# A decoder layer on one core: the activated MLP columns transposed by a trip through HBM and by VectorE in 32x32 blocks, and six pairs fewer by seven products

## The chip, the cores and the metric

One core of a Trainium2 chip runs the whole layer in one launch. The metric is the device time in microseconds of one execution; lower is better. The time before is the median of three runs.

## What is computed

A decoder layer over 256 tokens of width 2048, all in float32: two attention groups of eight heads each, an output projection with a residual, and an MLP. The change lies in the MLP alone:

```
h = _rmsnorm(x, norm_mlp_pre[layer])
u = jnp.square(jax.nn.relu(h @ w_up[layer]))
x = x + _rmsnorm(u @ w_down[layer], norm_mlp_post[layer])
```

Here h is 256x2048, `w_up` 2048x8192, u 256x8192 and `w_down` 8192x2048.

## The kernel before

**Exact products by three passes.** Each float32 operand is split into a part `hi` (float32r) and a rest `lo`. A product is three matmuls, hi*hi, hi*lo and lo*hi (`three`), each of 128 stationary columns and 512 moving ones. For each weight tile of 128x1024, ACT writes `hi` and DVE writes `lo` (`split`, and `split_gain` where the weights also take the RMSNorm gain).

**Up.** `w_up` is done in eight rounds j of 1024 columns (`for j in range(FF // CW)`). A round has four accumulators in PSUM, one for each of two token blocks b and two column halves n, and 16 steps over k, the blocks of 128 rows. A plain step ("k") is 4 products, 12 matmuls. Two neighbouring k steps can instead be a pair "by seven" ("w"): a Strassen-Winograd scheme with 7 products where the plain pair has 8. For that DVE forms sums of the weight blocks (`seven`: three additions of 128x1024 or 128x512), four pieces are split, and sums of the left operand are kept in `st` (`left_sums`). The extra products gather in four further banks m, and `close` and four additions bring them back into the accumulators at the round's end. `UP_STEPS` says which steps of a round go by seven, `UP_PAIRS` where the pair's weights are loaded to (`ab` and `ab2` through POOL's DMA queue, or two `raw` buffers through SP's).

**Evacuation of a round.** The down product needs u with its columns on the partitions. `up_evac` does this for each of the four accumulators: ACT writes `r` = Relu of the accumulator times the row scale, TensorE transposes `r` in four blocks of 128x128 into the accumulator's own bank (tile `rt`), and ACT squares that into `uT[j]` (a tile of 128x1024: 4 column blocks by 256 tokens). The banks then serve as m in the next round. For the column blocks in `AWAY`, `lo_away` also sends -hi to HBM by ACT's queue and adds u to it there by POOL's queue; the sum is the `lo` part, fetched again in down.

**Down.** `w_down` is done in two chunks of 1024 output columns, each over 64 k blocks, with the pairs of `DOWN_SEVEN` by seven; pairs in both lists (`SHARED`) form their left sums in the first chunk, keep them in HBM (`keep_s`) and fetch them in the second (`down_back`).

**Order.** The order on each engine and queue is the order of the calls; there is no scheduler. `Flow` keeps a clock that advances by TensorE's work as it is issued. A chain is a generator; `yield d` continues it d us of that clock later, so the delays (`D_UP`, `UP_STEP` and so on) place instructions in the queues of ACT, DVE, SP and POOL; the engines themselves wait for data by semaphores. `Weights.emit` issues loads and splits six tiles ahead of their use (`W_AHEAD`), with five `raw` buffers and eight pairs of hi and lo. Raw weight loads are on SP's queue:

```
raw = self.pool.tile([P, CW], F32, tag="raw", bufs=RAW_BUFS, name=name)
self.nc.sync.dma_start(out=out, in_=src)
```

Of the kernel before, what the change touches and what calls it, by code (L numbers as in the profile page):

```python
# [18 lines left out]
F32 = mybir.dt.float32  # L19
# [7 lines left out]
P = 128  # L27
D = 2048
# [61 lines left out]
D_X0, D_X, D_SS, D_TAB = 8.0, 3.0, 3.0, (14.0, 20.0)  # L90
D_NORM, D_HT, D_SECOND = 4.5, 1.5, 4.0

D_UP, UP_STEP = 1.8, 2.2


SUMS_AHEAD = 2


UP_PAIRS = [()] + [("ab", "ab2", "ab", "ab2")] * 5 + [("ab2", "ab", "raw", "ab"), ("ab", "raw", "raw")]


def up_steps(first, *groups):
# [4 lines left out]


THREE = up_steps(range(6, 11), (11, 12), (13,), (14, 15))
FOUR = up_steps(range(8, 12), (12,), (13,), (14,), (15,))  # L110
UP_STEPS = [up_steps(range(16)), THREE] + [FOUR] * 5 + [THREE]

ST = 13 * 256
N_SEVEN = [sum(w == "w" for w, _ in steps) for steps in UP_STEPS]


DOWN_SEVEN = ((5, 7, 9, 11, 13, 15, 19, 21, 23, 25, 27, 29), range(3, 28, 2))
AWAY = range(4, 14)
LATE = 10
SHARED = [k for k in DOWN_SEVEN[0] if k in DOWN_SEVEN[1]]  # L120
# [145 lines left out]
def layer(nc, tc, io):  # L266
# [13 lines left out]
    def bank(i, name):  # L280
        return ps.tile([P, 512], F32, tag=f"bank{i}", bufs=1, name=name)
# [650 lines left out]

    uT, ukeep = {}, {}

    def up_evac(j, b, i, acc, order):

        yield UP_STEP * order
        r = late["up"].tile([P, 512], F32, tag="r", bufs=2, name=f"r{j}_{b}")
        nc.scalar.activation(r, acc, AF.Relu, scale=rstd2[b])
        yield D_UP if j > 1 else 2 * D_UP  # L940
        t = bank(i, f"rt{j}_{b}")
        for k in range(4):
            transpose(t[:, k * P:(k + 1) * P], r[:, k * P:(k + 1) * P])
        if j not in uT:
            if j in (0, 1, 10, 11, 12, 13):
                t2 = late["u01" if j < 2 else "ab2" if j < 12 else "ab"][:, j % 2 * CW:(j % 2 + 1) * CW]
            else:
                tag = {"tag": "T", "bufs": 2} if j > 13 else {"tag": f"uT{j}", "bufs": 1}
                t2 = late["up"].tile([P, CW], F32, name=f"uT{j}", **tag)
            uT[j] = t2.rearrange("p (k s) -> p k s", k=4)  # L950
        nc.scalar.activation(uT[j][:, :, b * P:(b + 1) * P], t.rearrange("p (k s) -> p k s", k=4), AF.Square)
        if b and j in AWAY:
            flow.start(lo_away(j), 2.0 + 4.0 * (j % 2))

    def lo_away(g):

        ukeep[g] = dram.tile([P, CW], F32, name=f"ukeep{g}")
        u = uT[g].rearrange("p k s -> p (k s)")
        for h in range(2):
            c = slice(h * 512, (h + 1) * 512)  # L960
            t = late["up"].tile([P, 512], F32, tag="r", bufs=2, name=f"neg{g}_{h}")
            nc.scalar.activation(t.bitcast(F32R), u[:, c], AF.Copy, scale=-1.0)
            yield 1.0
            nc.scalar.dma_start(out=ukeep[g][:, c], in_=t)
            yield 7.0
        if g < LATE:
            yield 34.0
        else:
            while not dpl:
                yield 2.0  # L970
            yield 4.0 + 5.0 * (g % 2) + 20.0 * ((g - LATE) // 2)
        for h in range(2):
            c = slice(h * 512, (h + 1) * 512)
            nc.gpsimd.dma_start(out=ukeep[g][:, c], in_=u[:, c], accum_op=OP.add)
            yield 2.0 if g < LATE else 10.0

    def split_u(c, g):
        if (c, g) == (0, 0):
            uh, ul = [wp.tile([P, CW], F32R, tag=w, bufs=W_BUFS, name=f"u{w}0").rearrange("p (k s) -> p k s", k=4)
                      for w in ("hi", "lo")]  # L980
        else:
            uh = dpl["dp"].tile([P, 4, S], F32R, tag="uhi", bufs=2, name=f"uhi{c}_{g}")
            ul = u_lo.pop((c, g), None) or lo_tile(c, g)
        u, h, l = [x.rearrange("p k s -> p (k s)") for x in (uT[g], uh, ul)]
        if c and g or g in AWAY:
            nc.scalar.activation(h, u, AF.Copy)
            if not c:
                load_lo(c, g, ul)
        else:
            split(h, l, u)  # L990
        return uh, ul
# [99 lines left out]
    for j in range(FF // CW):  # L1091
        at = {bn: 4 * (j % 2) + i for i, bn in enumerate(PARTS)}
        if j == 0:
            accs = {bn: acc_bank(f"acc_u0_{bn[0]}{bn[1]}") for bn in at}
            at = {bn: (turn[0] - 3 + i) % 4 for i, bn in enumerate(at)}
        else:
            accs = {bn: bank(i, f"acc_u{j}_{bn[0]}{bn[1]}") for bn, i in at.items()}
        steps = wide_u[j]
        order = in_order(len(steps), (APART[1], 0)) if j == 0 else [(t, b) for t, (w, _, _) in enumerate(steps)
                                                                    for b in range(NB if w == "k" else 1)]  # L1100
        for t, b in order:
            what, k, tiles = steps[t]
            if (j, t, b) == (0, 8, 0):
                flow.finish(*res)
                late["po"].release()
                mix.release()
                late["up"] = pool("up", "right")
                late["st"] = late["up"].tile([P, ST], F32R, tag="st", bufs=1, name="st")
                for n in ("ab", "ab2", "c", "u01"):
                    late[n] = late["up"].tile([P, 2 * CW], F32, name=n)  # L1110
                flow.start(all_sums())
            if (j, t, b) == (FF // CW - 1, 4, 0):
                weights.limit -= 1
                u_next = split_u(0, 0)
            if (j, what, k, b) == (1, "k", 8, 0):
                fourth = flow.start(left_sums(3), 20.0)
            if j == 2 and t == 0:
                flow.finish(fourth)
            if j == 1 and what == "w":
                flow.until(lambda: len(sums) > k)  # L1120
            if what == "k":
                w = weights.get(tiles[0])
                h_done(k, b)
                for n in range(2):
                    c = slice(n * 512, (n + 1) * 512)
                    three(accs[b, n], [tok(hT[x], k, b) for x in range(2)], [w[x][:, 0, c] for x in range(2)], t == 0, t == len(steps) - 1)
                    if j == 0 and t == len(steps) - 1:
                        evac.append(flow.start(up_evac(n, b, at[b, n], accs[b, n], 2 * b + n - 0.25 * (2 * b + n))))
                    flow.pump()
                if b == NB - 1:  # L1130
                    weights.free(tiles[0])
                continue

            first, last = k == 0, k == N_SEVEN[j] - 1
            if first:
                weights.ahead = W_AHEAD
                flow.finish(*evac[-4:])
                m = {n: bank(i, f"m{n}_{j}") for n, i in zip((1, 6, 7, 5), free)}
            blocks = [[tok(hT[x], 2 * k + kk, bb) for x in range(2)] for kk, bb in ((0, 0), (1, 0), (1, 1))]
            if last:  # L1140
                weights.ahead -= 1
            seven_products(tiles, (blocks, sums[k]), accs, m, first, last, last and N_SEVEN[j] > 3)
            if last:
                more = close(closing(), m)
        free = [at[bn] for bn in PARTS]
        if j:

            for bn in PARTS:
                nc.vector.tensor_tensor(out=accs[bn], in0=accs[bn], in1=more[bn], op=OP.add)
            for o, (b, n) in enumerate(PARTS):  # L1150
                evac.append(flow.start(up_evac(2 * j + n, b, at[b, n], accs[b, n], o + 0.6)))
    weights.ahead = W_AHEAD
    u_last = evac[-4:]
    up = late["up"]
# [86 lines left out]
    for c in range(2):  # L1241
# [5 lines left out]
        for t, (what, k, tiles) in enumerate(wide_d[c]):  # L1247
# [31 lines left out]
            if (c, what, k) == (0, "k", 3):  # L1279
                weights.limit += 1  # L1280
            if (c, what, k) == (0, "k", 36):
                g_half = [late["up"].tile([P, 512], F32, tag="r", bufs=2, name=f"g_half{n}") for n in range(2)]
                for n in range(2):
                    load_gain(n, g_half[n])
            if (c, what, k) == (1, "k", 40):
# [39 lines left out]
def arrays_of(inputs):  # L1325

    a = {n: np.ascontiguousarray(inputs[n][0]) for n in ("x", "w_in", "w_uq", "w_ukv", "w_out", "w_up", "w_down")}
    a["xt"] = np.ascontiguousarray(np.concatenate([a["x"], inputs["norm_attn_pre"]]).T)
    a["pos"] = np.ascontiguousarray(inputs["positions"].reshape(NB, P).T)
    a["gains"] = np.ascontiguousarray(np.concatenate(  # L1330
        [inputs[n].reshape(-1, P) for n in ("q_latent_norm", "kv_latent_norm", "norm_mlp_pre")]).T)
    for n in ("norm_attn_post", "norm_mlp_post"):
        a[n] = np.ascontiguousarray(inputs[n])
    a["consts"] = shape_constants()
    return a
# [20 lines left out]
```

## Time and profile before

| | |
|---|---|
| median of three runs | 1046.23 us (1046.1 to 1047.08) |
| the profiled execution | 1045.28 us, of which the span is 1043.5 |
| granted TensorE clock | 0.998 |
| busy: PE, DVE, ACT, POOL | 99%, 81%, 62%, 8% of the span |
| the up rounds | from 368 to 702 us of the span |
| the down chunks | from 702 us on |
| transposes of `r` on PE (`rt`) | 128, between 403.0 and 714.2 us |

The profile is one execution seen by the hardware profiler. PE is TensorE's matmuls, PEld its weight loads, DVE VectorE, ACT ScalarE, POOL GpSimd, SP the engine that issues most of the DMAs. The lines by slices show the busy share of 40 equal parts of the span in tenths. L298 is the matmul helper, L302 the transpose helper, L308 and L309 the two instructions of a split, L312 and L313 those of a split with gain.

### The profile page before, as it was taken

How to read it: one execution, taken by the hardware profiler on the slowest of the kernel's cores; microseconds unless marked ns; L12 is line 12 of the kernel's file. 1: busy time of each engine (PE TensorE's matmuls, PEld its weight loads, DVE VectorE, ACT ScalarE, POOL GpSimd, SP SyncE). 2: the span in 40 equal slices, each digit the busy share in tenths (PEclk: the TensorE clock that was granted, in tenths of full speed). 3: DMA queues.
4: the chain of work that ended last, by engine and by line, in shares of the span. 5: the costliest groups of instructions: out<-in, count | busy, mean ns of one | idle time of the engine just before them, and what ended most of it. 6: DMA issues, size and time to landing. Idle time of an engine off the chain costs nothing.

```text
span 1043.5 us, 13429 instructions
## 1 busy us (share of the span) xinstructions
PE 1033.2 (99%) x4825; PEld 859.5 (82%) x4825; DVE 843.1 (81%) x1132; ACT 641.9 (62%) x876; POOL 79.8 (8%) x121
## 2 busy tenths in 40 slices
PE   9999999999999999999999999999999999999996
PEld 6888889888888888888888888888888888888885
DVE  6676536567547669999999999898998999898795
ACT  6584436565445566665866767666675765766561
POOL 0000000000000000000011101001101001111100
PEclk9999999999999999999999999999999999999999
DMA  9975447454447295646769668489979868888962
GB/s 308 362 233 150 139 131 241 145 162 151 151 148 239 99 350 184 225 150 205 228 213 316 174 245 247 147 289 324 348 255 357 288 226 329 294 313 318 364 223 81
DMA packets 86787, 244.02 MB, mean 234 GB/s; under 512 B 7616, under 2 KB 12224, under 8 KB 86336
## 3 DMA queue, kind: packets, MB, share of 16 engines
q1 hardware_dynamic: 62560, 164.13, 46.0%
q0 software_dynamic: 20848, 73.41, 22.1%
q10 hardware_dynamic: 3312, 5.62, 1.5%
q8 instruction: 38, 0.62, 0.2%
q14 instruction: 29, 0.24, 0.1%
HBM read 220.06 MB, written 23.07 MB: 233 GB/s over the span
## 4 chain that ended last, share of the span: by engine, by line
PE 96%; DVE 1%; issue 1%; DMA 0%; ACT 0%; SPq 0%; POOL 0%; DVEq 0%; POOLq 0%; ACTq 0%
PE y L298 24%; PE acc_u L298 24%; PE acc_o L298 8%; PE m L298 7%; PE md L298 7%; PE acc_v L298 4%; PE acc_qk L298 4%; PE acc_ckv L298 2%; PE acc_ukv L298 2%; PE acc_q L298 2%; PE acc_cq L298 2%; PE acc_k L298 2%; PE acc_uq L298 2%; PE rt L302 1%; PE sc_b L298 1%
## 5 line engine op out<-in xcount | busy, mean ns | idle before, releaser
L309 DVE TENSOR_TENSOR lo<-raw,hi 128x1024 fp32r<-128x1024 f32 (+3 forms) x205 | 231.2, 1148 | 79.3 <-ACT hi L308 78.5
L308 ACT ACTIVATE hi<-raw 128x1024 fp32r<-128x1024 f32 (+3 forms) x205 | 201.5, 996 | 70.7 <-DMA raw<-in_w_in 16.5
L298 PE MATMUL acc_u<-hi,hT_hi 128*128 128x512 f32 x356 | 141.6, 398 | 0.0
L298 PE MATMUL acc_u<-hi,hT_lo 128*128 128x512 f32 x356 | 139.1, 391 | 0.4 <-DVE hT_lo L309 0.4
L298 PE MATMUL acc_u<-lo,hT_hi 128*128 128x512 f32 x356 | 138.8, 390 | 0.0
L298 PE MATMUL y<-hi,uhi 128*128 128x512 f32 x346 | 135.0, 390 | 0.0
L298 PE MATMUL y<-hi,ulo 128*128 128x512 f32 x346 | 134.7, 389 | 0.0
L298 PE MATMUL y<-lo,uhi 128*128 128x512 f32 x346 | 134.6, 389 | 0.0
L313 DVE SCALAR_TENSOR_TENSOR lo<-raw,gcol,hi 128x1024 fp32r<-128x1024 f32 x74 | 92.4, 1279 | 9.6 <-ACT hi L312 9.5
L312 ACT ACTIVATE hi<-raw,gcol 128x1024 fp32r<-128x1024 f32 x74 | 83.0, 1146 | 26.2 <-DMA raw<-in_w_up 13.1
L298 PEld LDWEIGHTS acc_u<-hi,hT_lo 128*128 128x128 f32 x356 | 66.8, 188 | 14.9 <-DVE hT_lo L309 0.9
L298 PEld LDWEIGHTS acc_u<-lo,hT_hi 128*128 128x128 f32 x356 | 67.0, 188 | 12.9
L298 PEld LDWEIGHTS acc_u<-hi,hT_hi 128*128 128x128 f32 x356 | 66.9, 188 | 12.8
L298 PEld LDWEIGHTS y<-hi,uhi 128*128 128x128 f32 x346 | 65.0, 188 | 13.4
L298 PEld LDWEIGHTS y<-hi,ulo 128*128 128x128 f32 x346 | 65.0, 188 | 13.4
L298 PEld LDWEIGHTS y<-lo,uhi 128*128 128x128 f32 x346 | 65.0, 188 | 13.4
L308 ACT ACTIVATE hi<-u 128x1024 fp32r<-128x1024 f32 (+1 forms) x38 | 37.6, 991 | 46.1 <-DVE u L368 30.5
L309 DVE TENSOR_TENSOR lo<-st_down,hi 128x1024 fp32r<-128x1024 f32 x50 | 59.9, 1220 | 1.1 <-ACT hi L308 1.1
L308 ACT ACTIVATE hi<-st_down 128x1024 fp32r<-128x1024 f32 x50 | 52.0, 1049 | 5.8 <-PE y L298 4.1
L298 PE MATMUL md<-hi,s 128*128 128x512 f32 x150 | 54.3, 389 | 0.0
L298 PE MATMUL acc_o<-hi,mixT_hi 128*128 128x512 f32 x128 | 51.8, 405 | 0.0
L298 PE MATMUL acc_o<-hi,mixT_lo 128*128 128x512 f32 x128 | 50.2, 392 | 0.0
(332 smaller groups left out, 2167.7 us busy)
## 6 DMA issues: line engine op xcount, KB each, us to landing
raw<-in_w_down SPq DMA_DIRECT2D x78, 512.0 KB, 6.5
raw<-in_w_up SPq DMA_DIRECT2D x76, 512.0 KB, 5.3
raw<-in_w_in SPq DMA_DIRECT2D x55, 512.0 KB, 4.8
ab<-in_w_up POOLq DMA_DIRECT2D x22, 1024.0 KB, 5.9
raw<-in_w_out SPq DMA_DIRECT2D x32, 512.0 KB, 4.2
ab_down<-in_w_down POOLq DMA_DIRECT2D x13, 1024.0 KB, 9.2
ulo<-ukeep POOLq DMA_DIRECT2D x25, 512.0 KB, 6.0
c<-in_w_down POOLq DMA_DIRECT2D x6, 1024.0 KB, 10.8
```

Source lines behind the costliest of these rows:

```text
L298: nc.tensor.matmul(out, a, b, start=start, stop=stop)
L302: nc.tensor.transpose(out, a, ident)
L308: nc.scalar.activation(hi, src, AF.Copy)
L309: nc.vector.tensor_tensor(out=lo, in0=src, in1=hi.bitcast(F32), op=OP.subtract)
L312: nc.scalar.activation(hi, src, AF.Copy, scale=g)
L313: nc.vector.scalar_tensor_tensor(out=lo, in0=src, scalar=g, in1=hi.bitcast(F32), op0=OP.mult, op1=OP.subtract)
```

## The change

- `up_evac` no longer transposes. After Relu, ACT squares `r` in place in SBUF and writes it to a tile in HBM (`rkeep`, 128 tokens x 512 columns, 256 KB) by its own queue. It then starts `turn_u`.
- `turn_u`, 9 us of the flow's clock later (11 for the last of a round's four), reads that tile back by four DMAs on SP's queue. Each fills 32 partitions: the tokens of a block of 32 go on the partitions and the runs of 128 columns stay whole (512 bytes), so that 32x32 blocks stand where a transpose of each block alone gives the transposed tile. 7 us later VectorE does one transpose of 128x512 in 32x32 blocks into `uT[j]`.
- Each group of 128 columns of u then stands on the partitions in another order, so the rows of `w_down` are permuted likewise on the host.
- Every up round from the second on has three pairs by seven (before: 3, 4, 4, 4, 4, 4, 3), and the first down chunk loses the pair 5. The fourth pair's left sums are no longer made. The space they had is the third buffer of tag `r`, which now holds `r`, the read-back tile `x` and the negated copies of `lo_away` in turn.
- The delays in `lo_away` become shorter (7 to 4 twice, 34 to 26), as it starts later.
- `split_u` waits, in the order of issue, until a tile's transposes have been issued.

```
-D_UP, UP_STEP = 1.8, 2.2
+UP_STEP = 2.4
+D_BACK, D_TURN, D_LO, D_ADD = 9.0, 7.0, 4.0, 26.0
...
-UP_PAIRS = [()] + [("ab", "ab2", "ab", "ab2")] * 5 + [("ab2", "ab", "raw", "ab"), ("ab", "raw", "raw")]
+UP_PAIRS = [(), *[("ab", "ab2", "ab"), ("ab2", "ab", "ab2")] * 2, ("ab", "ab2", "ab"), ("ab2", "ab", "raw"),
+            ("ab", "raw", "raw")]
...
 THREE = up_steps(range(6, 11), (11, 12), (13,), (14, 15))
-FOUR = up_steps(range(8, 12), (12,), (13,), (14,), (15,))
-UP_STEPS = [up_steps(range(16)), THREE] + [FOUR] * 5 + [THREE]
-
-ST = 13 * 256
+UP_STEPS = [up_steps(range(16))] + [THREE] * 7
+
+ST = 10 * 256
...
-DOWN_SEVEN = ((5, 7, 9, 11, 13, 15, 19, 21, 23, 25, 27, 29), range(3, 28, 2))
+DOWN_SEVEN = ((7, 9, 11, 13, 15, 19, 21, 23, 25, 27, 29), range(3, 28, 2))
...
-    def up_evac(j, b, i, acc, order):
+    def up_evac(j, b, acc, order):
 
         yield UP_STEP * order
-        r = late["up"].tile([P, 512], F32, tag="r", bufs=2, name=f"r{j}_{b}")
+        r = late["up"].tile([P, 512], F32, tag="r", bufs=3, name=f"r{j}_{b}")
         nc.scalar.activation(r, acc, AF.Relu, scale=rstd2[b])
-        yield D_UP if j > 1 else 2 * D_UP
-        t = bank(i, f"rt{j}_{b}")
-        for k in range(4):
-            transpose(t[:, k * P:(k + 1) * P], r[:, k * P:(k + 1) * P])
+        nc.scalar.activation(r, r, AF.Square)
+        keep = dram.tile([P, 512], F32, name=f"rkeep{j}_{b}")
+        nc.scalar.dma_start(out=keep, in_=r)
+        flow.start(turn_u(j, b, keep), D_BACK + 2.0 * (b and j % 2))
+
+    turned = set()
+
+    def turn_u(j, b, keep):
+
+        x = late["up"].tile([P, 512], F32, tag="r", bufs=3, name=f"x{j}_{b}")
+        back = keep.rearrange("(q t) (a c) -> a t q c", q=4, a=4)
+        for a in range(4):
+            nc.sync.dma_start(out=x[32 * a:32 * a + 32].rearrange("t (q c) -> t q c", q=4), in_=back[a])
+        yield D_TURN
...
-        nc.scalar.activation(uT[j][:, :, b * P:(b + 1) * P], t.rearrange("p (k s) -> p k s", k=4), AF.Square)
-        if b and j in AWAY:
-            flow.start(lo_away(j), 2.0 + 4.0 * (j % 2))
+        nc.vector.transpose(uT[j][:, :, b * P:(b + 1) * P].rearrange("p k (q t) -> p k q t", q=4),
+                            x.rearrange("p (q k c) -> p k q c", q=4, k=4))
+        if b:
+            turned.add(j)
+            if j in AWAY:
+                flow.start(lo_away(j), 1.0)
...
-            yield 7.0
+            yield D_LO
         if g < LATE:
-            yield 34.0
+            yield D_ADD
...
     def split_u(c, g):
+        flow.until(lambda: g in turned)
...
-            if (j, what, k, b) == (1, "k", 8, 0):
-                fourth = flow.start(left_sums(3), 20.0)
-            if j == 2 and t == 0:
-                flow.finish(fourth)
...
+    a["w_down"] = np.ascontiguousarray(
+        a["w_down"].reshape(FF // 512, 4, 4, 32, D).transpose(0, 2, 1, 3, 4).reshape(FF, D))
```

More of the change, by code (lines that the diff above doesn't have):

```diff
@@ L960, in lo_away @@
             c = slice(h * 512, (h + 1) * 512)
-            t = late["up"].tile([P, 512], F32, tag="r", bufs=2, name=f"neg{g}_{h}")
+            t = late["up"].tile([P, 512], F32, tag="r", bufs=3, name=f"neg{g}_{h}")
             nc.scalar.activation(t.bitcast(F32R), u[:, c], AF.Copy, scale=-1.0)
@@ L1127, in layer @@
                     if j == 0 and t == len(steps) - 1:
-                        evac.append(flow.start(up_evac(n, b, at[b, n], accs[b, n], 2 * b + n - 0.25 * (2 * b + n))))
+                        evac.append(flow.start(up_evac(n, b, accs[b, n], 0.75 * (2 * b + n))))
                     flow.pump()
@@ L1150, in layer @@
             for o, (b, n) in enumerate(PARTS):
-                evac.append(flow.start(up_evac(2 * j + n, b, at[b, n], accs[b, n], o + 0.6)))
+                evac.append(flow.start(up_evac(2 * j + n, b, accs[b, n], o + 0.6)))
     weights.ahead = W_AHEAD
@@ L1281, in layer @@
             if (c, what, k) == (0, "k", 36):
-                g_half = [late["up"].tile([P, 512], F32, tag="r", bufs=2, name=f"g_half{n}") for n in range(2)]
+                g_half = [late["up"].tile([P, 512], F32, tag="r", bufs=3, name=f"g_half{n}") for n in range(2)]
                 for n in range(2):
```

## The prediction

> **What bounds the kernel now.** I read the page first, then TensorE's waits, then the chain in order of time, and last the stage around the change, round by round.
>
> ```profile
> span 1043.5 us, 13429 instructions
> PE 1033.2 (99%) x4825; PEld 859.5 (82%) x4825; DVE 843.1 (81%) x1132; ACT 641.9 (62%) x876; POOL 79.8 (8%) x121
> PE   9999999999999999999999999999999999999996
> DVE  6676536567547669999999999898998999898795
> DMA  9975447454447295646769668489979868888962
> ```
>
> The share for DVE, 81%, is a mean over two halves. In the attention half it is idle for a third or more of the time; in the MLP half, where the change lies, it shows nines. PE shows nines everywhere but at the very end. So I ask what PE waited for:
>
> ```profile
> PE warm L523 <- DVE zero L520: 1.2, 1, 1.2
> PE acc_u L298 <- DVE hT_lo L309: 0.4, 1, 0.4
> PE qrt L302 <- DVE qT L774: 0.2, 1, 0.2
> ```
>
> That is the whole list: 1.8 us, none of it inside the up rounds or the down chunks. There the time is what PE issues; an instruction taken off PE shortens the run by its own time, until another engine cannot follow.
>
> The chain gives the price of a matmul and the length of a round:
>
> ```profile
> 525.19 9.52 PE acc_u L298 x42
> 568.07 9.52 PE acc_u L298 x42
> 610.93 9.52 PE acc_u L298 x42
> 653.79 9.52 PE acc_u L298 x42
> 859.10 27.20 PE y L298 x120
> ```
>
> 27.20/120 = 0.2267 us for a matmul of 512 columns. The run of 42 stands at the same place of each round, so a round of four products-by-seven lasts 42.86 us. It has 16 x 12 - 4 x 3 = 180 matmuls, 40.80 us. The other 2.06 us are its 16 transposes, in four groups, and what they disturb. The same chain inside a round shows two groups themselves:
>
> ```profile
> 577.60 0.44 PE rt L302 x4
> 580.12 0.59 PE rt L302 x4
> ```
>
> **The change part by part.**
>
> *128 transposes leave PE* (32 groups of four). By the shorter group, 32 x 0.44 = 14.1 us; by what a round lasts beyond its matmuls, 8 x 2.06 = 16.5 us, which also holds the slightly slower matmuls between the groups. I take 16.5, since the round is measured whole, and keep 14.1.
>
> *Six pairs return from seven products to eight.* The rounds of before have 0, 3, 4, 4, 4, 4, 4, 3 such pairs, those of after 0 and seven times 3: five fewer. Down's first chunk loses pair 5. Each gives back one product of three passes: 6 x 3 x 0.2267 = +4.1 us.
>
> *The evacuation on ACT.* Before, Relu and a Square out of PSUM; now Relu, a Square in SBUF and a DMA issue.
>
> ```profile
> L939 ACT ACTIVATE r<-acc_u,rstd_pre 128x512 f32<-128x512 f32 x4 | 2.6, 688 | 3.4 <-DVE acc_u L1149 3.4
> L962 ACT ACTIVATE neg<-uT 128x512 fp32r<-128x512 f32 x4 | 2.5, 623 | 1.4 <-DMA ukeep<-neg 1.4
> L951 ACT ACTIVATE uT<-rt 128x512 f32<-128x512 f32 x4 | 2.4, 601 | 0.5 <-PE rt L302 0.5
> L964 ACTq DMA_DIRECT2D ukeep<-neg x20: 326/327/342, 500.5 to 689.2; - x20
> ```
>
> The new Square is like the copy of L962 (623 ns against 601), and the issue costs 0.33 us: 4 x 0.35 = 1.4 us more for ACT in a round, where it is busy some 30 of 43 us (windows below). Zero on the path. The bank comes free after Relu instead of after the second Square, while the first product that needs it moves from after four k steps to after five (13.6 us), so m's wait cannot grow by this. Without that cover PE would wait for the last Relu of each round.
>
> *DVE: 32 block transposes in, six pairs' sums and splits out.*
>
> ```profile
> 535.00:577.00 42.00, 42.00 (x193) 34.48 (x192) 40.17 (x44) 29.73 (x37) 6.60 (x8) 1.00 0.81 251
> 577.00:620.00 43.00, 43.00 (x198) 35.37 (x197) 41.15 (x45) 29.72 (x37) 7.52 (x9) 1.00 0.82 250
> 620.00:663.00 43.00, 43.00 (x198) 35.30 (x198) 41.22 (x46) 31.06 (x39) 5.04 (x6) 1.00 0.74 233
> 720.00:760.00 40.00, 40.00 (x178) 33.15 (x177) 37.46 (x48) 23.78 (x28) 6.38 (x9) 1.00 1.01 346
> ```
>
> Columns: stretch, its length, then busy time of PE, its weight loads, DVE, ACT and POOL, the granted clock, the DMA share and GB/s. DVE has under 2 us free in a round. The forms of the first stretch:
>
> ```profile
> L313 DVE SCALAR_TENSOR_TENSOR lo<-raw,gcol,hi 128x1024 fp32r<-128x1024 f32 x8 | 9.9, 1278 | 0.0
> L309 DVE TENSOR_TENSOR lo<-u,hi 128x1024 fp32r<-128x1024 f32 x4 | 4.9, 1220 | 0.1
> L309 DVE TENSOR_TENSOR lo<-t,hi 128x1024 fp32r<-128x1024 f32 x4 | 4.9, 1220 | 0.8 <-ACT hi L308 0.8
> L309 DVE TENSOR_TENSOR lo<-ab,hi 128x1024 fp32r<-128x1024 f32 x4 | 4.9, 1219 | 0.3 <-ACT hi L308 0.3
> L363 DVE TENSOR_TENSOR t<-ab 128x1024 f32<-128x1024 f32 x4 | 4.9, 1218 | 0.0
> L368 DVE TENSOR_TENSOR u<-u,ab 128x512 f32<-128x512 f32 x4 | 2.8, 692 | 0.1
> L367 DVE TENSOR_TENSOR u<-t,ab 128x512 f32<-128x512 f32 x4 | 2.8, 692 | 0.1
> L309 DVE TENSOR_TENSOR lo<-ab,hi 128x512 fp32r<-128x512 f32 x4 | 2.7, 686 | 0.3 <-ACT hi L308 0.3
> L1083 DVE TENSOR_TENSOR c<-m,c 128x512 f32<-128x512 f32 x4 | 2.7, 687 | 0.2
> L1149 DVE TENSOR_TENSOR acc_u<-acc_u,c 128x512 f32<-128x512 f32 x4 | 2.5, 691 | 0.0
> ```
>
> They sum to 43.0 us; their ends overlap, so the engine is busy 40.17, a factor of 0.934. A pair costs a quarter of rows two to eight, 27.9/4 = 7.0; a plain k step 9.9/8 = 1.24. With three pairs and ten k steps: 12.4 + 20.9 + 5.2 = 38.5, times 0.934 = 36.0 us. No row shows a block transpose. The nearest are the passes of 512 columns at 0.69; the far end is the slowest form here, 1.28, as if every element took twice as long. I take 0.69: 36.0 + 4 x 0.65 = 38.6 us in a round of 183 x 0.2267 = 41.5. So DVE goes from 1.7 us free to 2.9; at 1.28 it has 40.8, still inside. Price on the path: zero, cover 2.9 us; DVE becomes the bound when a transpose takes over (41.5 - 36.0)/(4 x 0.934) = 1.47 us. The Trainium skill (VectorE: DVE Perf Modes, The three transpose paths) gives 311 ns for 128x128 in blocks on VectorE; four of those would be an estimate of 1.24 us for 512 columns, by which the sum stays as it is and the free time shrinks to 0.9 us. No run here shows it yet.
>
> *The trip through HBM.* 32 writes of 256 KB on ACT's queue, then 32 x 4 reads on SP's queue in runs of 512 bytes (128 columns).
>
> ```profile
> q10 hardware_dynamic: 3312, 5.62, 1.5%
> raw<-in_w_up SPq DMA_DIRECT2D x76, 512.0 KB, 5.3
> ukeep<-neg ACTq DMA_DIRECT2D x20, 256.0 KB, 4.1
> ukeep<-ab POOLq DMA_DIRECT2D x8, 256.0 KB, 14.1
> ```
>
> ACT's queue took 1.5% of 16 x 1043.5 us for 3312 packets: 76 ns each, nearly all of 2 KB. A read packet of 512 bytes lies between a quarter of that, 19 ns, and all of it. A tile has 512: 0.6 to 2.4 us on 16 engines; with its write (128 x 76/16 = 0.6) 5 to 12 us of DMA a round. The rounds use up to 0.82 of 43 us, so 8 are free; at the costly end the fullest two run over by 4. Near the low end, as I take it, all fits: in bytes, 2.1 MB in 41.5 us add 50 GB/s to 250, and 720 to 760 shows 346 moved. The Trainium skill (DMA: Bandwidth & Descriptors, Specifications) puts the least size for line rate at 512 bytes, which is this size; by it the low end holds.
>
> Latency: each read is queued 9 us after its Relu, each transpose 7 us later. The write should land 4.1 us after issue, and the read, as large, after about as long. On SP the raw weight loads stand behind a read that waits for its write; ACT's splits, DVE's, then PE wait for them. Five raw buffers cover this, 4 x 1.24 us of DVE work and more. Behind a late transpose on DVE stand the splits. How far those run ahead of PE in the tightest place:
>
> ```profile
> 605.57 1.22 DVE L309 TENSOR_TENSOR lo<-t,hi 128x1024 fp32r<-128x1024 f32 x1
> 609.18 0.61 PE L298 MATMUL m<-hi,st 128*128 128x512 f32 x2
> ```
>
> The last split of a round ends at 606.8 and is first used in the second matmul of the lower row, 609.4: 2.6 us ahead, although it was put on the queue some six tiles ahead. DVE thus reaches a transpose later than the plan counts, which gives the read more time. Price zero; bounds: no gain below that (the transposed tile's first use is in down), and above it the slower rivals below.
>
> *The rest at zero.* The negated copies start some 12 us later, but their waits shrink (7 to 4 twice, 34 to 26), so POOL's adding DMAs stand within 2 us of where they stood (59 us after a round's end) among its 1 MB weight loads. The fourth pair of left sums goes from DVE in round 1. Weights 6 and 7 get the gain form in six rounds, counted at 1.24. In down, pair 5's sums move from chunk 0 to chunk 1, where they replace a load; both are outside PE's path, as DVE has 2.5 us of 40 free. Four tiles fall into 702 to 760 where DMA is full (1.01): 2 MB, 6 us at 346 GB/s, covered by the raw buffers and the split tiles, against a 1 MB pair load that now starts later.
>
> Sum, against the profiled execution's 1045.28 us (span 1043.5 and 1.8 around it): -16.5 + 4.1 = -12.4, 1032.9. It ran 0.95 below the median of 1046.23, so on the median's scale **1033.8**; with 14.1 for the transposes, 1036.2.
>
> **The rivals.**
>
> *The read-back comes late (slower).* DVE is in order, so a tile that lands late holds up the splits. If a read took 14.1 us from issue, as the accumulating writes do, instead of the 7 planned, each round would lose 7.1 - 2.9 = 4.2 us, eight times 34: 1068. It turns the result at 2.9 + 12.4/8 = 4.4 us of lateness, a landing of 11.4 us. For it: DMA at 0.8 and a write, a read and two queues in series. Against: 256 KB landed in 4.1 us in these rounds, and DVE's own lag.
>
> *Strided access is slow in itself (slower).* With the packets at four times the upper price, 304 ns, a tile takes 9.7 us, four take 39 of a round with 8 free: 31 us late in each, 1034 + 8 x 31 = 1280. The Trainium skill (VectorE: DVE Perf Modes, The three transpose paths) warns that a transpose by access-pattern strides in a DMA is 19 times slower when the inner stride is large. Here the inner run is 512 bytes on both sides, which speaks against.
>
> *DVE becomes the bound (slower).* At 2.5 us a transpose, DVE needs 36.0 + 9.3 = 45.3 a round, 3.8 too many, seven times: 1061. For it: no row of the operation; against: the far end of the rows fits.
>
> *Part is given back.* Short waits, up to 1.2 us in a round and a few more where down begins and DMA is full: 1037 to 1044.
>
> **How the numbers follow.** The sum holds, 1031 to 1037: 0.66. Part given back, 1037 to 1044: 0.14. Within 0.2%, about what a measurement of this kernel tells from no change (2.1 us, 1044.1 to 1048.3): 0.06, all of the gain gone to waits. Slower: late read-back 0.08, DVE bound 0.05, strided access 0.01. So faster 0.80, same 0.06, slower 0.14. The range for eight in ten, 1030 to 1045, leaves out the slower cases and most of the middle one.
>
> **What would show it.** Right: no transposes on PE in the up rounds; rounds of 41.5 us; PE's list of waits still a few us; block transposes near 0.69 us; DVE at some 39 of 41.5. Wrong: acc_u or m waiting for DVE lo, DVE idle before the transposes with a DMA as releaser, SP waiting long at the reads, or block transposes over 1.5 us.

## The result and the profile after

The changed kernel takes 1108.8 us (median of four runs, 1107.6 to 1110.5) against 1046.5 for the kernel before on the same chip: ratio 1.0596, 95% interval [1.0578, 1.0615]. It is 62 us slower where 12 us faster were forecast. The page of after, the lines that were shown of before and one more (PEclk, the granted TensorE clock in tenths, which was all nines before):

```profile
span 1105.8 us, 13478 instructions
PE 1051.4 (95%) x4715; PEld 862.3 (78%) x4715; DVE 836.4 (76%) x1125; ACT 638.1 (58%) x862; POOL 74.7 (7%) x114
PE   9999999999999998999889889899799999999997
DVE  6776457567465696888778688787689899999795
PEclk9999999999999998999989999999899999999999
DMA  9965456454283756575686796769897968798972
```

PE now has gaps in slices 16 to 29, where the up rounds and the start of down lie. DVE is busy for less time than before (836 against 843), so it is not the bound. What PE waited for in that stretch:

```profile
PE acc_u L300 <- ACT hi L314: 12.1, 4, 4.3
PE acc_u L300 <- ACT c L1096: 9.2, 5, 3.5
PE acc_u L300 <- DVE lo L315: 7.2, 9, 1.9
```

The first and the third row are the two halves of the splits of raw weights (L314, L315). The second is ACT's copy of a bank m in `close`, which stands on ACT's queue behind such splits. Going one step back, ACT waited for the raw loads, and SP, which issues these, waited at the new reads (L954):

```profile
ACT hi L314 <- DMA raw<-in_w_up: 86.8, 37, 8.6
```

```profile
SPq L954 <- DMA rkeep<-r: 139.0, 23, 16.4
SPq L954 <- DVE uT L963: 40.4, 5, 8.8
SPq L954 <- DVE ab L963: 16.3, 2, 8.3
SPq L954 <- DVE u L963: 6.5, 1, 6.5
```

Columns of a wait: us in total, times, longest. Two kinds of wait stand at the reads: 139 us for a write of `r`, and 63 us (three rows) for VectorE's transpose of an earlier tile, which frees the buffer of tag `r` that the read fills. The chain in one round shows the path whole:

```profile
554.93 0.64 ACT r L942
555.60 2.01 DMA rkeep<-r
557.62 0.03 SPq L954
...
559.07 0.43 SPq L954
559.50 0.04 issue
559.55 10.64 DMA raw<-in_w_up
...
570.27 1.16 ACT hi L314
```

Square, write to HBM, the four reads on SP (1.8 us), and only then a raw load, which takes 10.6 us to land (the median is 6.2); ACT splits it as it lands. SP's own timeline shows how long it stood there:

```profile
529.27 13.30 SPq L194 DMA_DIRECT2D raw<-in_w_up  x8
557.75 1.75 SPq L954 DMA_DIRECT2D x<-rkeep  x4
```

Its raw loads were issued by 542.6, and it came to the reads then, 9 us before ACT began the round's first Relu (551.5) and 15 us before it could go on. The write that let it go on is that of the round's second tile, whose Relu starts at 554.2, and not that of the first, which these reads fetch: by the order of calls with three buffers of tag `r`, the first read fills the buffer that the second `r` held.

PE had run dry meanwhile, and the gap costs twice:

```profile
567.80 0.39 PE L300 MATMUL acc_u<-hi,hT_lo 128*128 128x512 f32 x1
571.47 0.51 PE L300 MATMUL acc_u<-hi,hT_hi 128*128 128x512 f32 x1 [3.29 <-ACT hi L314]
...
573.81 0.63 PE L300 MATMUL acc_u<-hi,hT_hi 128*128 128x512 f32 x1
...
577.23 0.63 PE L300 MATMUL acc_u<-hi,hT_lo 128*128 128x512 f32 x1
```

```profile
567.00:569.00 2.00, 1.19 (x6) 0.64 (x4) 0.00 (x0) 0.00 (x0) 0.00 (x0) 1.00 1.08 322
573.00:575.00 2.00, 2.00 (x5) 1.61 (x6) 2.00 (x3) 1.78 (x2) 0.22 (x1) 0.50 1.13 245
579.00:581.00 2.00, 2.00 (x10) 1.64 (x9) 2.00 (x3) 1.25 (x2) 0.00 (x0) 1.00 0.25 100
```

After 3.3 us idle the granted clock is 0.50 (the column after the busy times); eight matmuls take 3.42 us, 0.43 each for 0.227, until it is 1.00 again by 579. The Trainium skill (TensorE: Matmul & The Clock Gate, Why this matters for your kernels) asks for no idle gaps of TensorE over about 3 us; this gap agrees. A shorter one in the same trace shows that 3 us is no safe limit here: 2.20 us of idle were followed by a clock of 0.50 too, while 1.92 us (before the matmul at 723.12) were not.

```profile
817.17 0.50 PE L300 MATMUL y<-lo,uhi 128*128 128x512 f32 x1 [2.20 <-DVE lo L311]
819.00:821.00 2.00, 2.00 (x6) 1.54 (x6) 1.93 (x5) 0.00 (x0) 0.70 (x1) 0.50 0.46 170
```

### The profile page after: what moved, and what is told of

It is laid out like the page before. It is cut to its first block, busy times and chain, and to the rows that moved or that the text cites. A ratio compares the mean times of both kernels' runs of the same rounds, so it can differ in the third digit from the quotient of the medians.

```text
span 1105.8 us, 13478 instructions
## 1 busy us (share of the span) xinstructions
PE 1051.4 (95%) x4715; PEld 862.3 (78%) x4715; DVE 836.4 (76%) x1125; ACT 638.1 (58%) x862; POOL 74.7 (7%) x114
## 4 chain that ended last, share of the span: by engine, by line
PE 60%; DMA 16%; DVE 10%; issue 5%; ACT 5%; SPq 2%; ACTq 0%; POOL 0%; DVEq 0%; POOLq 0%
PE y L300 19%; DMA raw<-in_w_up 8%; PE acc_o L300 8%; PE md L300 5%; PE acc_v L300 4%; PE acc_u L300 4%; PE acc_qk L300 4%; DVE lo L315 3%; DVE lo L311 2%; PE acc_ckv L300 2%; DMA ukeep<-neg 2%; PE acc_ukv L300 2%; PE acc_q L300 2%; PE acc_cq L300 2%; PE acc_k L300 2%
## 5 line engine op out<-in xcount | busy, mean ns | idle before, releaser
L310 ACT ACTIVATE hi<-raw 128x1024 fp32r<-128x1024 f32 (+3 forms) x205 | 201.0, 995 | 77.0 <-DMA raw<-in_w_down 21.6
L300 PE MATMUL acc_u<-hi,hT_hi 128*128 128x512 f32 x386 | 158.2, 410 | 24.2 <-ACT hi L314 12.1
L300 PE MATMUL acc_u<-lo,hT_hi 128*128 128x512 f32 x386 | 157.3, 408 | 7.2 <-DVE lo L315 7.2
L315 DVE SCALAR_TENSOR_TENSOR lo<-raw,gcol,hi 128x1024 fp32r<-128x1024 f32 x86 | 108.5, 1280 | 63.8 <-ACT hi L314 63.6
L300 PE MATMUL acc_u<-hi,hT_lo 128*128 128x512 f32 x386 | 155.8, 404 | 0.4 <-DVE hT_lo L311 0.4
L314 ACT ACTIVATE hi<-raw,gcol 128x1024 fp32r<-128x1024 f32 x86 | 97.4, 1148 | 93.6 <-DMA raw<-in_w_up 86.8
L300 PE MATMUL y<-hi,uhi 128*128 128x512 f32 x352 | 139.7, 397 | 3.7 <-ACT c L1096 1.6
L300 PEld LDWEIGHTS acc_u<-hi,hT_hi 128*128 128x128 f32 x386 | 75.4, 195 | 47.6 <-ACT hi L314 14.1
L300 PEld LDWEIGHTS acc_u<-lo,hT_hi 128*128 128x128 f32 x386 | 76.0, 197 | 26.6 <-DVE lo L315 11.8
L300 PEld LDWEIGHTS acc_u<-hi,hT_lo 128*128 128x128 f32 x386 | 75.7, 196 | 16.8 <-DVE hT_lo L311 0.9
L300 PEld LDWEIGHTS y<-hi,ulo 128*128 128x128 f32 x352 | 67.3, 191 | 21.6 <-DVE ulo L311 7.3
L310 ACT ACTIVATE hi<-st_down 128x1024 fp32r<-128x1024 f32 x48 | 49.8, 1048 | 4.6 <-DVE st_down L370 3.1
L300 PE MATMUL acc_o<-lo,mixT_hi 128*128 128x512 f32 x128 | 50.0, 390 | 0.0
```

Of the source, the lines that this page charges most:

```text
L300: nc.tensor.matmul(out, a, b, start=start, stop=stop)
L310: nc.scalar.activation(hi, src, AF.Copy)
L314: nc.scalar.activation(hi, src, AF.Copy, scale=g)
L315: nc.vector.scalar_tensor_tensor(out=lo, in0=src, scalar=g, in1=hi.bitcast(F32), op0=OP.mult, op1=OP.subtract)
```

## The experiments

The theories at the start: **queue** (SP stands at a read that cannot start yet, and raw loads behind it come late) and **traffic** (the trip's bytes and short packets make the raw loads land late). Times are medians; a difference is between medians. The ratio is to the kernel before, run beside it on the same chip, and brackets hold its 95% interval.

**The sum by itself, and the first moves**

`e4_no_trip`:

```
-D_BACK, D_TURN, D_LO, D_ADD = 9.0, 7.0, 4.0, 26.0
+D_BACK, D_TURN, D_LO, D_ADD = 0.0, 3.0, 4.0, 26.0
...
-        keep = dram.tile([P, 512], F32, name=f"rkeep{j}_{b}")
-        nc.scalar.dma_start(out=keep, in_=r)
-        flow.start(turn_u(j, b, keep), D_BACK + 2.0 * (b and j % 2))
+        flow.start(turn_u(j, b, r), D_BACK)
```

> The changed kernel without the trip: VectorE transposes the 32x32 blocks straight from r, 3 us of the flow's clock after it was asked for; nothing is written to or read from HBM and the moving of the blocks is left out. All else (no transposes on TensorE, six pairs fewer, DVE's 32 block transposes) stays. If the prediction's sum of TensorE and its zero for DVE are right: 1031 to 1037. If DVE's transposes or the new order of the evacuation cost by themselves: above 1046.

Measured 1035.6, ratio 0.9903 [0.9888, 0.9918]. Its rounds last 41.48 us, 183 x 0.2267 to the hundredth:

```profile
420.72 5.44 PE acc_u L300 x24
...
462.20 5.44 PE acc_u L300 x24
...
503.68 5.44 PE acc_u L300 x24
```

So PE's sum and the zeros for DVE and the evacuation hold within 2 us. The whole loss, 73.2 us, is the trip.

`e5_six_fewer`: before with the new `UP_STEPS`, `UP_PAIRS` and `DOWN_SEVEN` alone.

> The kernel before with only the six pairs fewer by seven (three pairs in each round, first down chunk without pair 5); TensorE still transposes. By the prediction's term, 18 matmuls of 0.2267 us more: +4.1 us, 1050 to 1051. If fewer pairs upset or ease DVE and the loads as well, it lies outside 1048 to 1053.

Measured 1049.4, ratio 1.0033 [1.0021, 1.0044]: +3.5, and 4.1 lies within the interval.

`e1_reads_act`: `nc.sync` to `nc.scalar` at the reads.

> The changed kernel with its 128 reads of the trip issued from ACT's queue, not SP's; same bytes, same runs of 512 bytes, same delays. Queue theory (a read stands on SP's queue before its write has landed, SP waits there 139 us in all, and the raw weight loads behind it come late): ACT gets to a read some 9 us after its own Relu, when the write (3.5 us to landing) is down, so the waits of SP for rkeep go, ACT's 86.8 us of waits for raw weights fall under 20, and the time falls by 50 to 75 us from 1108.8, to 1034 to 1058. Traffic theory (the trip's bytes and short packets load the DMA engines, and raw weights land late for that: 6.2 us against 5.3): as slow as the changed kernel, 1095 to 1110.

Measured 1102.1, ratio 1.0538 [1.0522, 1.0554]. SP no longer stands at the reads, but now ACT does:

```profile
ACT hi L310 <- DMA x<-rkeep: 29.4, 10, 7.6
ACT hi L310 <- DVE uT L963: 24.0, 4, 6.0
```

One step of the queue theory held: ACT's waits for raw weights in up (L314) fell from 86.8 to 10.4 us. Its time failed, because ACT is not paced by the planning clock either. It ran the late Relus and the reads in one burst (a write issued at 453.75 us, the first four reads from 454.20 on), so the reads still stood ahead of their data and the splits behind them. It tells nothing for traffic, since the wait only moved.

`e3_whole_rows`: `nc.sync.dma_start(out=x, in_=keep)` for the four reads.

> The changed kernel with each tile read back by one DMA in rows of 2 KB instead of four DMAs in runs of 512 bytes, at the same place on SP's queue; it leaves out the moving of the 32-wide blocks, so later values are other ones. Queue theory: SP still waits for the write; three issues fewer (1.3 us of SP per tile) help a little: 1090 to 1109. Traffic theory: the short packets were the cost, and the time falls below 1070.

Measured 1093.2 (two runs), ratio 1.0450 [1.0429, 1.0471], 16 us less: inside the queue theory's range and far from 1070. SP waited longer than in the changed kernel (164 us for `rkeep`) and the time still fell, so reading in four DMAs of short runs has a price of its own.

**Remedies on the changed kernel**

`e6_old_tile`: `back` is a view of the first tile written, for all tiles but the two of the first 512 columns. `e7_old_tile_four`: that with `bufs=4` at tag `r` (the scratch tile of down's squares moves into the tag to make room, here and in e8).

> The changed kernel, same queue, place, bytes and runs, but from the second tile on each read fetches the tile that the first evacuation wrote, long landed, so no read waits for its own write (the values are those of another tile). Queue theory: SP's 139 us of waits for rkeep go, those for a free buffer (63 us) stay or grow: 1050 to 1085. Traffic theory (the trip's load on the DMA engines): the same traffic, 1095 to 1110.

> As e6_old_tile, with four buffers of tag r in place of three, so that a read no longer waits for VectorE's transpose of the tile before it either. Queue theory: SP has no wait left at the reads, 1034 to 1050; what stays above e4_no_trip (1035.6) is the price of the traffic itself. Traffic theory: above 1080.

Measured 1109.1 [1.0579, 1.0622] and 1084.3 [1.0314, 1.0413], two runs each. Both missed what they were made for: SP waited for `rkeep` 134 and 136 us. A read's buffer was the `r` of an evacuation, so it still waited for a write, for the buffer and not for the data. This bears on the changed kernel too: taking away the wait for the data alone changed neither SP's wait nor the time. What else is left of the pair: with four buffers no read waited for a transpose any more, and 25 us went.

`e2_reads_later`: `D_BACK` 22 for 9. `e8_later_four`: that with four buffers.

> The changed kernel with each read put on SP's queue 22 us of the flow's clock after its Relu in place of 9, all else the same. Queue theory: the write has landed by then in nearly all rounds (SP waited 16.4 us at most): rkeep waits under 30 us, but with three buffers the fourth read still waits for the first's transpose: 1045 to 1085. If the wait only moves: above 1095.

> Both remedies: reads 22 us after the Relu and four buffers; a complete kernel. Queue theory: both waits of SP gone, 1034 to 1048, faster than the kernel before if the raw weights land in time. Traffic theory: above 1080.

Measured 1079.4 [1.0296, 1.0338] and 1060.0 [1.0107, 1.0141]: 29 and 49 us less than the changed kernel, two thirds of the trip's cost with both. So waiting is the larger part. Neither got rid of it: in e2 SP still waited 90 us for writes where under 30 were expected, and e8, which missed its 1048 and is still slower than before, waited for writes and now for negated copies, which share tag `r`:

```profile
SPq L954 <- DMA rkeep<-r: 70.9, 16, 13.1
SPq L954 <- DMA ukeep<-neg: 34.4, 4, 14.8
```

`e14_pool_own`: reads by `nc.gpsimd`, tag `x` with two buffers, `r` with two, `D_BACK + 1.8 * (2 * b + j % 2)`. `e16_sp_own_later`: the same buffers and spacing on SP, `D_BACK` 22.

> A complete kernel: the reads on POOL's queue, where the pairs' 1 MB loads wait for VectorE anyway, into two buffers of their own, r with two; reads 9 us after the Relu, then spaced by 4 us. Queue theory: raw weights on SP come in time; the pair loads behind a read are late by a few us and are used later than raw ones: 1036 to 1060. If any in-order queue of weights passes the wait on as SP's and ACT's did: above 1080.

> As e8_later_four, reads on SP's queue 22 us after the Relu, but with two buffers for r and two for the read tile, and the reads spaced by 4 us, so that a read waits neither for a later write nor for a negated copy (34 us in e8). Queue theory: less waiting on SP than e8's 105 us at the reads, 1036 to 1058. Traffic theory: no better than e8's 1060.

Measured 1097.7 [1.0474, 1.0506] and 1160.4 [1.1070, 1.1103]. On POOL the reads stand as they did on SP, now ahead of the pair loads, the first row for the write, the second for a transpose (two buffers of `r` also cost something by themselves, as e21 shows below):

```profile
POOL x L954 <- DMA rkeep<-r: 114.8, 7, 24.2
...
POOL x L954 <- DVE uT L963: 66.1, 5, 13.3
```

And e16, made to wait less, is the slowest of all. With two buffers each read needs the transpose of the tile two before it, put on DVE's queue only 1.4 us of the planning clock earlier:

```profile
SPq L954 <- DVE uT L963: 129.2, 11, 22.0
SPq L954 <- DVE ab L963: 37.6, 4, 10.1
SPq L954 <- DVE u L963: 26.6, 2, 21.4
```

This is a ring: the read waits for DVE, DVE stands at splits that come before the transpose in its order, and their raw weights stand behind the read on SP. The other two links show in the waits from 395 to 830 us: DVE waited 122 us for ACT's halves of splits (18 in e4), and ACT 78 us for raw loads (32 in e4).

**Waits without traffic, traffic without waits** (all on e4_no_trip)

`e12_wait_only`:

```
+        keep = dram.tile([P, 8], F32, name=f"rkeep{j}_{b}")
+        nc.scalar.dma_start(out=keep, in_=r[:, :8])
+        flow.start(turn_u(j, b, r), D_BACK)
+        flow.start(small_read(j, b, keep), 9.0 + 2.0 * (b and j % 2))
```

> e4_no_trip (1035.6) with a small trip beside it: ACT writes 8 columns of r (4 KB, not 256) to HBM, and four reads of that stand on SP's queue where the changed kernel's reads stand, 9 us after the Relu, into a spare strip that nothing uses. So SP waits for each evacuation's write, but hardly a byte moves; no buffer of the trip is waited for. Queue theory: the wait is the cost; SP waits some 100 us at the reads, raw weights come late, 1060 to 1095. Traffic theory: 1034 to 1042.

Measured 1042.3, ratio 0.9958 [0.9941, 0.9974]: +6.7 only, although SP waited nearly as long as in the changed kernel:

```profile
SPq L951 <- DMA rkeep<-r: 124.9, 23, 13.9
SPq L194 <- DVE lo L315: 97.3, 41, 5.8
```

The forecast of the queue theory failed again. The second row shows where the time was taken from: it is SP's wait for a `raw` buffer to come free, which in e4 is 265.8 us. SP had time to spare and stood at the reads instead. The sum of its waits is no measure of their cost.

`e19_wait_turn`, and `e20_both_waits` with e12's reads as well:

```
+        if not b and not j % 2:
+            flow.start(late_turn(j), 16.0)
...
+        nc.vector.tensor_copy(pad[:, :8], uT[j][:, 0, :8])
+        yield 2.2
+        out = dram.tile([P, 8], F32, name=f"pad_out{j}")
+        nc.sync.dma_start(out=out, in_=pad[:, :8])
```

> e4_no_trip (1035.6) with one small store on SP's queue in each round that waits for a small DVE copy (8 columns), put on DVE's queue where the changed kernel's first transpose of a round stands; the store stands where its fourth read stands, 2.2 us of the clock later. This is the changed kernel's wait of SP for a buffer that a transpose frees, without traffic and without the wait for a write. If that wait makes the gap from e7 (four buffers, 1084) to the changed kernel (1109) by itself: 1050 to 1065. If it costs only where the raw loads are slow already: 1035 to 1042.

> e12_wait_only (1042.3) and e19's store together: both of SP's waits, no traffic to speak of. If waits add up, e12 plus what e19 adds. If they multiply, since each takes from the same lead of five raw buffers: more than the sum, 1065 to 1085, and the traffic's own part of the 73 us would be the smaller one.

Measured 1057.9 [1.0095, 1.0125], +22.3, and 1072.0 [1.0232, 1.0262], +36.4 where the sum would be 29.0. Waiting for DVE's queue once in a round cost three times the wait for four writes, and the two do more than add. But e19 by itself is a larger dose than it was meant to be: SP stood at its eight stores for 181 us, against 63 us at transposes in the changed kernel. In e20 the dose is near the changed kernel's. The first row is e19's, the other two are e20's:

```profile
SPq L952 <- DVE con_pad L949: 181.3, 8, 29.2
...
SPq L961 <- DMA rkeep<-r: 123.8, 22, 13.8
SPq L956 <- DVE row L953: 50.7, 8, 8.7
```

In e20 that is 174 us against 202. This places 36 of the 73 us on the two waits, with hardly a byte moved.

`e13_traffic_only`: every `r` written whole, 256 KB read in runs of 512 bytes from the first tile into two spare buffers; `r` has two. `e17_traffic_rows`: the reads as one DMA in rows of 2 KB. `e18_writes_only`: no reads. `e21_two_buffers`: neither, `r` with two. `e22_writes_three`: the writes, `r` with three.

> e4_no_trip with the whole traffic of the trip and without its wait: every r is written to HBM, and 256 KB are read in runs of 512 bytes at the same places of SP's queue, but from the tile that the first evacuation wrote, into two buffers of their own that nothing uses, so a read waits at most for the read two before it. Tag r has two buffers here. Queue theory: 1036 to 1055. Traffic theory: above 1070. (It is what e6 and e7 were meant to be: there the read's buffer was r's, and so its wait for the write stayed.)

> e13_traffic_only (1061.6) with each 256 KB read as one DMA in rows of 2 KB, not four in runs of 512 bytes: same bytes, a quarter of the packets and of the issues. If the short packets are the traffic's cost (39 ns each by the growth of SP's queue from e4 to e13, 5 us of 16 engines in a round): 1040 to 1050. If the bytes or the place on the queue are: 1056 to 1064.

> e13_traffic_only without its reads: the 32 writes of 256 KB stay on ACT's queue, and tag r has two buffers as there. If the reads carry the traffic's cost: 1035 to 1042. If the writes, or r's two buffers (a Relu then waits for the write two before it), carry it: 1048 to 1062.

> e18_writes_only (1049.8) without its 32 writes: no trip at all, tag r with two buffers. If the writes cost the 14 us over e4_no_trip: 1035 to 1038. If the two buffers do (ACT waited 7.7 us there for transposes before a Relu, with the splits behind it): 1046 to 1051.

> e4_no_trip with the 32 writes of 256 KB on ACT's queue and its three buffers of tag r. If the writes cost: 1046 to 1050. If the two buffers did: 1035 to 1039.

| | reads | writes | buffers of r | us | ratio to before |
|---|---|---|---|---|---|
| e4 | none | none | 3 | 1035.6 | [0.9888, 0.9918] |
| e22 | none | 256 KB | 3 | 1039.8 | [0.9927, 0.9960] |
| e21 | none | none | 2 | 1046.4 | [0.9996, 1.0015] |
| e18 | none | 256 KB | 2 | 1049.8 | [1.0022, 1.0061] |
| e17 | rows of 2 KB | 256 KB | 2 | 1054.5 | [1.0051, 1.0102] |
| e13 | runs of 512 B | 256 KB | 2 | 1061.6 | [1.0132, 1.0162] |

Of e13's 26 us, 10.8 come from taking a buffer from `r`, a side effect of the edit and no part of the trip's traffic: ACT then waits for a transpose before it can write a Relu. The traffic is 15.2: writes some 4, reads 5 as rows, 7 more for cutting them in short runs, in four DMAs for one; no run parts the runs from the three issues more. (e13 and e17 came out between the ranges of their theories. They are not quite free of waiting either: SP stood at their reads for 75 and 73 us, mostly for earlier DMAs.) SP's queue shows the price of a run (packets, MB, share of 16 engines' span):

```profile
q1 hardware_dynamic: 64144, 169.90, 48.3%
```

```profile
q1 hardware_dynamic: 82576, 178.30, 50.9%
```

```profile
q1 hardware_dynamic: 68752, 178.29, 49.5%
```

These are e4, e13 and e17. From e4 to e13, 16 x (50.9% of 1060.3 - 48.3% of 1034.3) = 642 us for 18432 packets, 35 ns each; to e17, 16 x (49.5% of 1053.2 - 48.3% of 1034.3) = 348 us for 4608, 76 ns. The counts hold some packets beyond the 16384 runs and 4096 rows of data; by run and by row it is 39 and 85 ns. The same bytes take 1.85 times the engines' time in runs of 512 bytes.

**What stays open.** Traffic 15.2 and waits 36.4 make 51.6 of the 73.2 us. The other 21.6 appear only when both are there. That each worsens the other is seen twice (whole rows save 16 us in the changed kernel, 7 without its waits; the remedies save 49 where the waits alone cost 36), but no run divides these 21.6, and waits of ACT for transposes before the negated copies (26 us in the changed kernel) were not tried apart. More `raw` buffers, the direct test of SP's lead, were not tried either. No complete kernel with the trip beat the kernel before; the nearest, e8, is at 1.0124 [1.0107, 1.0141].

## Why the prediction was wrong

*The sum on PE* was right: -16.5 + 4.1 gave 1033.8, and without the trip the kernel takes 1035.6. From e5 to e4, which takes the transposes off PE, 13.8 us go, which is nearer to the 14.1 that the prediction kept aside than to the 16.5 that it took. (One small misreading did no harm: the 0.4 us that PE waited at acc_u, at 366.4 us, lie inside the first up round, whose matmuls begin at 354.3.)

*DVE at zero* was right. The block transpose takes what the rows of 512 columns suggested, and not the estimate of 1.24 us from the Trainium skill (VectorE: DVE Perf Modes, The three transpose paths), whose 311 ns are given for bfloat16, where this tile is float32; the measurement decides:

```profile
L963 DVE STREAM_TRANSPOSE uT<-x x20: 669/702/705, 478.5 to 795.3; 128x512 f32<-128x512 f32 x20
```

*The trip at zero* failed, in four places.

1. "Five raw buffers cover this". I had named the right thing, raw loads behind a read that waits for a write, and then priced it as if SP came to the read at the planning clock's time. SP does not follow that clock. It runs ahead of DVE as far as its buffers allow, while ACT's Relu waits for DVE (20 us in all at L941); so it stood there for 139 us, 16.4 the longest. The Trainium skill (DMA: Bandwidth & Descriptors, Anatomy of one DMA) says that the wait happens on the issuing sequencer and not in the DMA engines; L954's rows agree. By itself the cover all but held: such a wait of 125 us cost 6.7 us (e12). It failed together with the next two.

2. The third buffer of tag `r`. The prediction costed its space and not its rotation. By the order of calls the first three reads need buffers of later evacuations, so they wait for those writes as well (e6), and a fourth read needs the buffer of the first, which only DVE frees, far back in its own order. Four buffers took 25 us off (e6 to e7); such a wait alone, without traffic but longer, made 22 (e19), and with the wait for writes 36 (e20).

3. "Near the low end, as I take it, all fits". A short packet took 35 ns, in the middle of my 19 to 76, and the rule of the Trainium skill (DMA: Bandwidth & Descriptors, Specifications) that 512 bytes reach line rate led me to the wrong end. The measurement decides: here the same bytes in rows of 2 KB took half the time. The writes and reads cost some 15 us by themselves.

4. The price of a gap. I counted a wait of PE at its length. The same 4715 matmuls keep PE busy 1051.4 us here and 1022.0 in e4: of the 71.5 us between the two spans, 42.1 are idle and 29.4 are matmuls at a lower clock.

*The rivals.* "The read-back comes late" had the right place and the wrong queue: DVE never waited for a tile (the trip's DMAs landed in some 3 us, sooner than I assumed); SP waited to issue them. I had argued it away with a landing time, which does not contain the wait ahead of the issue, and gave it too small a chance.

## What to carry to other kernels

Before a DMA that depends on fresh data goes onto a queue of prefetches, ask when that queue's engine will really come to it (as early as its free buffers let it), and what frees the buffer it fills; if that is an engine whose own work is fed from behind the DMA, the ring costs more than the wait seems to. Moving the DMA to another in-order queue moved the wait to whatever stood there, on ACT's queue (e1) as on POOL's (e14). And count a gap on TensorE of some 2 us or more at up to twice its length: in the changed kernel 42 us of idle came with 29 us of slower matmuls.

## What the runs showed that I had not expected

- SP waiting 125 us at 128 small reads cost 6.7 us (e12), while waiting 181 us at eight stores cost 22.3 (e19). One stay was 29.2 us at the longest there, and 13.9 in e12; that a long stay empties the `raw` buffers where short ones do not is the likely reason, and not shown.
- Reads from HBM in runs of 512 bytes: 35 ns a packet against 76 ns in rows of 2 KB, for a quarter of the bytes.
- One idle gap of TensorE of 3.3 us was followed by some 6 us at a granted clock of 0.50, and one of 2.2 us by over 3 us at 0.50.
- One buffer less for a tile that ACT fills and DVE empties cost 10.8 us, with no DMA in the trip at all (e21).
